# Attention scores from 64-row matmuls on undoubled operands, in a two-layer decoder kernel

## The chip, the cores and the metric

The kernel runs on one core of a Trainium2 chip. The metric is the device time of one execution in microseconds (us), the lower the better. One launch computes everything below.

## What is computed

Two decoder layers, for a prompt of 1024 tokens and for 8 sampled tokens with a paged cache. Each layer projects the normalized input and splits it over two groups of heads: four heads of differential attention and four heads of gated linear attention. Both groups feed one output projection, which a SwiGLU block follows. The change lies in the attention of the prompt. Each of its heads has two maps of queries and keys, 64 wide, and values 128 wide:

```python
def diff_attn_prompt(q, k, v, lam):
    ...
    scale = DIFF_DK ** -0.5
    ...
    def one_block(args):
        qi, i = args
        s = jnp.einsum('bqhmd,bkhmd->bhmqk', qi, k).astype(jnp.float32) * scale
        ...
        p = jax.nn.softmax(jnp.where(mask, s, -jnp.inf), axis=-1)
        w = p[:, :, 0] - lam * p[:, :, 1]
        return jnp.einsum('bhqk,bkhv->bqhv', w.astype(v.dtype), v)
```

Here `m` runs over the two maps, `q` over the queries of a block of 128, `k` over the keys, and the mask lets a query see the keys up to its own position.

## The kernel before

Each layer goes through three stages. `phase_d` does the differential attention of the prompt, `phase_g` the gated linear attention, and the last and longest stage the output projection and the feed-forward block in two halves, with the decoding of the samples mixed into the first. `phase_d` takes roughly the first 300 us of each layer.

To keep accuracy, matrices are split into a high part, rounded to the fast matmul format (F32R), and a low part, the rest. A product is then the sum of high times high, low times high and high times low. A projection (`gemm_tok`) does this with three matmuls for each of eight slices of the input.

In `phase_d`, each of the four heads prepares its weights (`prep_cols`: a copy on ScalarE, ACT, and a subtraction on VectorE, DVE) and then walks over eight tiles of 128 tokens and one of the samples. `proj(i)` projects tile i into the PSUM tile `psq`, normalizes and rotates queries and keys on ACT and DVE, transposes them on TensorE (PE) into the PSUM tile `tpqk`, and lays them out as operands: rows 0 to 63 come from map 0, rows 64 to 127 from map 1. `attend(i)` follows two tiles behind (`LAG`). It multiplies the queries of tile i with all keys up to tile i, in pieces of up to 512 keys, so tiles 0 to 3 have one piece and tiles 4 to 7 two. Each piece of a map goes into a PSUM tile `psS` of a pool of three (tag `S`), from which one DVE operation (line 504) adds the mask, scales, and keeps a running extreme in `mx`. ACT then takes the exponential of the row, the maps are combined, PE transposes the result (`tpw`, into `wT`) and multiplies it with the values (`po`, in full precision, two matmul instructions for each call).

The layout of the operands is where the change lies. A score of one map needs a contraction over 64 rows only. The kernel before fills all 128 rows of the array instead: `qhh` holds the high part of a map's queries twice, once in each half of the rows, and `kt` holds the high part of that map's keys in one half and the low part in the other. One matmul (line 500) then gives high times high plus high times low. A second one (line 501) takes the low part of the queries, `ql`, against the same keys. It is zero in the other half; for that, four tiles `qlz` are zeroed by GpSimd (POOL) at the start of the stage (lines 579 to 582) and only their live halves are written. So a piece of a map takes two matmuls of 128 rows, and a tile's operands take four ACT copies (lines 471, 475, 476, 481) and four DVE subtractions of 64 rows (lines 474, 482, 483).

The order on each engine isn't written out by hand in this stage. Instructions carry a priority in program order, and a planner places each engine's instructions before the launch by priority and readiness under its own estimate of durations. An instruction that isn't ready lets others pass it in the plan, and on the chip each engine then keeps to the plan. So matmuls of later projections stand between those of scores, transposes and `po`.

Two other matmuls of the kernel use less than the whole array and are spoken of below. `puG` in `phase_g` (line 794) writes 64 columns at a time, the lower and the upper half in turn, in full precision. `psw` in the decoding (line 1182) contracts over 64 rows and gives 32 columns of result.

Of the kernel before, what the change touches and what calls it, by code (L numbers as in the profile page):

```python
# [10 lines left out]
F32 = mybir.dt.float32  # L11
F32R = mybir.dt.float32r
# [3 lines left out]
AF = mybir.ActivationFunctionType  # L16
ALU = mybir.AluOpType
# [4 lines left out]
P = 128  # L22
DM = 1024
KD = DM // P
SEQ = 1024
# [15 lines left out]
DK = 64  # L41
# [3 lines left out]
LAG = 2  # L45
# [9 lines left out]
BIG = 3.0e38  # L55


def f(ap):
    return ap.bitcast(F32)
# [3 lines left out]
def hybrid_kernel(  # L63
# [8 lines left out]
    PE, ACT, DVE, POOL, SP = nc.tensor, nc.scalar, nc.vector, nc.gpsimd, nc.sync  # L72
# [8 lines left out]
    def mm(out, lhsT, rhs, start, stop):  # L81
        PE.matmul(out, lhsT=lhsT, rhs=rhs, start=start, stop=stop, skip_group_check=True)  # L82
# [4 lines left out]
    def act(out, in_, func, **kw):  # L87
        return ACT.activation(out, in_, func, **kw)  # L88
# [45 lines left out]
    def tt(out, a, b, op, eng=None):  # L134
        return (eng or DVE).tensor_tensor(out, a, b, op=op)  # L135
# [4 lines left out]
    def bc(ap, shape):  # L140
        return ap.to_broadcast(shape)
# [242 lines left out]
    def phase_d(l, dctx, sn, pgp):  # L384
# [8 lines left out]
        dp = Two()  # L393
# [9 lines left out]
        def head(h):  # L403
# [3 lines left out]
            kt = [None, None]  # L407
# [4 lines left out]
            def proj(i):  # L412
                n = P if i < NT else NB
                ps = psg.tile([P, 512], F32, name="psq", tag="g")
                gemm_tok(ps, nc_, Hs, Ls, i)
                if i == NT:
                    z = dp.tile([NB, 384 + RANK], F32, name="zs", tag="zs", bufs=1)
                    z2 = dp.tile([P, 512], F32, name="zs2", tag="sqo", bufs=1)[0:NB, :nc_]
                    DVE.tensor_copy(z2, ps[32:32 + NB, :nc_])
                    tt(z[:, :nc_], ps[0:NB, :nc_], z2, ALU.add)  # L420
                    src = z
                else:
                    src = ps
                qn = pp.tile([P, 256], F32, name="qn", tag="qn", bufs=2)
                ms = pp.tile([P, 4], F32, name="ms", tag="ms", bufs=2)
                for a in range(4):
                    act(qn[:n, a * DK:(a + 1) * DK], src[:n, a * DK:(a + 1) * DK], AF.Square, accum_out=ms[:n, a:a + 1])
                act(ms[:n], ms[:n], AF.Ln, scale=r2[:n, i:i + 1], bias=eps_t[:n])
                rs = pp.tile([P, 4], F32, name="rs", tag="rs", bufs=2)
                act(rs[:n], ms[:n], AF.Exp, scale=-0.5, bias=lnr[:n, i:i + 1])  # L430
                t2 = pp.tile([P, 256], F32, name="t2", tag="t2", bufs=1)
                qk = pp.tile([P, 256], F32, name="qk", tag="t1", bufs=2)
                v4 = "p (a d) -> p a d"
                v22 = "p (a m d) -> p a m d"
                vr = "p (a s d) -> p a s d"
                qs = src[:n, 0:256].rearrange(v22, a=2, m=2)
                tt(qk[:n].rearrange(v22, a=2, m=2), qs, bc(cg[:n, i, :, :].unsqueeze(2), [n, 2, 2, DK]), ALU.mult)
                tt(t2[:n].rearrange(v22, a=2, m=2), qs, bc(sg[:n, i, :, :].unsqueeze(2), [n, 2, 2, DK]), ALU.mult)
                tt(qk[:n].rearrange(vr, a=4, s=2), qk[:n].rearrange(vr, a=4, s=2),
                   t2[:n].rearrange(vr, a=4, s=2)[:, :, ::-1, :], ALU.add)  # L440
                tt(qk[:n].rearrange(v4, a=4), qk[:n].rearrange(v4, a=4), bc(rs[:n].unsqueeze(2), [n, 4, DK]), ALU.mult)
                v = dp.tile([P, DV], F32, name="v", tag="v", bufs=10)
                act(v[:n], src[:n, 256:384], AF.Copy, scale=rcol[:n, i:i + 1])
                if has_gr:
                    grt = pp.tile([P, RANK], F32, name="grt", tag="grt", bufs=2)
                    act(grt[:n], src[:n, 384:nc_], AF.Copy, scale=rcol[:n, i:i + 1])
                if i == NT:
                    if has_gr:
                        tp = psT.tile([P, 512], F32, name="tpgr", tag="T")
                        pe_t(tp[0:RANK, 0:NB], grt[0:NB], NB)  # L450
                        act(ssq[0:RANK, SEQ:TOK], tp[0:RANK, 0:NB], AF.Copy)
                    SP.dma_start(scr_q[l][:, h * P:(h + 1) * P], qk[:n, 0:128])
                    SP.dma_start(k_sample[l, :, h * P:(h + 1) * P], qk[:n, 128:256])
                    SP.dma_start(v_sample[l, :, h * P:(h + 1) * P], v[:n])
                    tt(z[:, 0:128], qk[:n, 0:128], qk[:n, 128:256], ALU.mult)
                    DVE.tensor_reduce(out=sn[:, 2 * h:2 * h + 2], in_=z[:, 0:128].rearrange("p (m d) -> p m d", m=2), axis=AX.X, op=ALU.add)
                    SP.dma_start(scr_v[l][:, h * P:(h + 1) * P], v[:n])
                    return None
                SP.dma_start(k_prompt[l, i * P:(i + 1) * P, h, :], qk[:, 128:256])
                SP.dma_start(v_prompt[l, i * P:(i + 1) * P, h, :], v)  # L460
                vts.append(v)
                tp = psT.tile([P, 512], F32, name="tpqk", tag="T")
                pe_t(tp[:, 0:128], qk[:, 0:128], P)
                pe_t(tp[:, 128:256], qk[:, 128:256], P)
                if has_gr:
                    pe_t(tp[0:RANK, 256:384], grt, P)
                    act(ssq[0:RANK, i * P:(i + 1) * P], tp[0:RANK, 256:384], AF.Copy)
                qhh = dp.tile([P, 2, P], F32R, name="qhh", tag="qhh", bufs=LAG + 2)
                ql = qlz[nql[0] % len(qlz)]
                nql[0] += 1  # L470
                act(qhh, bc(tp[:, 0:128].unsqueeze(1), [P, 2, P]), AF.Copy)
                for m in range(2):
                    r = slice(64 * m, 64 * m + 64)
                    tt(ql[r, m, :], tp[r, 0:128], f(qhh[r, m, :]), ALU.subtract)
                act(qhh[64:128, 0, :], tp[0:64, 0:128], AF.Copy)
                act(qhh[0:64, 1, :], tp[64:128, 0:128], AF.Copy)
                if i % 4 == 0:
                    kt[i // 4] = dp.tile([P, 2, 512], F32R, name="kt", tag="kt", bufs=3)
                kk = kt[i // 4]
                c = slice((i % 4) * P, (i % 4 + 1) * P)  # L480
                act(kk[:, :, c], bc(tp[:, 128:256].unsqueeze(1), [P, 2, P]), AF.Copy)
                tt(kk[64:128, 0, c], tp[0:64, 128:256], f(kk[0:64, 0, c]), ALU.subtract)
                tt(kk[0:64, 1, c], tp[64:128, 128:256], f(kk[64:128, 1, c]), ALU.subtract)
                qts[i] = (qhh, ql)

            wTs = []

            def attend(i):
                qhh, ql = qts.pop(i)
                n = (i + 1) * P  # L490
                sms = dp.tile([P, 2], F32, name="sms", tag="sms")
                scs = []
                for m in range(2):
                    sc = dp.tile([P, SEQ], F32, name="sc", tag="sc", bufs=4)
                    mx = dp.tile([P, 2], F32, name="mx", tag="mx", bufs=3)
                    for pi in range(0, n, 512):
                        w = min(512, n - pi)
                        ps = psS.tile([P, 512], F32, name="psS", tag="S")
                        kk = kt[pi // 512]
                        mm(ps[:, :w], qhh[:, m, :], kk[:, m, :w], True, False)  # L500
                        mm(ps[:, :w], ql[:, m, :], kk[:, m, :w], False, True)
                        o = SEQ - n + pi
                        q = pi // 512
                        DVE.tensor_tensor_reduce(
                            out=sc[:, pi:pi + w], in0=ps[:, :w], in1=mb[:, o:o + w], scale=-(DK ** -0.5),
                            scalar=BIG if q == 0 else mx[:, 0:1], op0=ALU.add, op1=ALU.min, accum_out=mx[:, q:q + 1])
                    q = (n - 1) // 512
                    act(sc[:, :n], sc[:, :n], AF.Exp, scale=-1.0, bias=mx[:, q:q + 1], accum_out=sms[:, m:m + 1])
                    scs.append(sc)
                rr = dp.tile([P, 2], F32, name="rr", tag="rr")  # L510
                DVE.reciprocal(rr, sms)
                tt(rr, rr, coef[:, l, :], ALU.mult)
# [63 lines left out]
        POOL.affine_select(out=mb[:, SEQ - P:], in_=mb[:, SEQ - P:], pattern=[[-1, P]], base=0,  # L576
                           channel_multiplier=1, compare_op=ALU.is_ge, fill=-1.0e30)

        nql = [0]
        qlz = [dp.tile([P, 2, P], F32R, name=f"qlz{z}", tag=f"qlz{z}", bufs=1) for z in range(LAG + 2)]  # L580
        for z in qlz:
            POOL.memset(f(z), 0.0)
        wa2 = pgp.tile([RANK, 256], F32, name="wa2", tag="wa2")
        POOL.dma_start(wa2, w_a2[l])
        pending = []
# [747 lines left out]
```

## Time and profile before

| | |
|---|---|
| median of three runs | 2788.39 us (2784.14 to 2790.25) |
| the profiled execution | 2795.14 us |
| its span, first to last instruction | 2793.3 us |
| mean granted clock of TensorE | 0.989 of full speed |
| PE busy | 2709.5 us, 97% of the span |
| ACT busy | 1358.8 us, 49% |
| DVE busy | 1824.9 us, 65% |
| POOL busy | 403.0 us, 14% |

A row of the profile names the line of the kernel (that of a helper, where one records the operation: L82 is every matmul, L85 every transpose, L88 every ACT operation, L135 a DVE operation on two tensors), the engine, the operation, and what is written and read by the program's names. PE is the matmul, PEld the load of its weights, which may run ahead of it. A matmul's shape is written as rows by columns of the array, then the size of what streams through it. The ends of matmuls are modelled: each lasts longer than the slot it takes in the stream, so successive ones overlap, and the distance between two starts is the better measure of what one costs. A row with a count in the timeline merges successive instructions of one kind, from the first start to the last end.

### The profile page before, as it was taken

What the parts mean: (1) busy time and instruction counts of PE and PEld (TensorE: products, weight loads), DVE (VectorE), ACT (ScalarE), POOL (GpSimd) and SP (SyncE); (2) the same over time, 40 slices, a digit from 0 to 9 for tenths busy, and PEclk for the clock granted to TensorE, in tenths of its full rate; (3) what the DMA queues carried; (4) which work ended last, traced back from release to release, by engine and by line L of the source; (5) the groups of instructions that cost most, each with busy time, mean ns of one, the idle gap of its engine ahead of it and who ended that gap; (6) DMA issues with size and microseconds to landing.
All of it is one profiled execution on the core that took longest, in us unless ns stands there. A gap on an engine that the chain in (4) does not pass through costs nothing.

```text
span 2793.3 us, 46822 instructions
## 1 busy us (share of the span) xinstructions
PE 2709.5 (97%) x16906; PEld 2403.9 (86%) x16906; DVE 1824.9 (65%) x3549; ACT 1358.8 (49%) x3343; POOL 403.0 (14%) x333
## 2 busy tenths in 40 slices
PE   8999999999999999999999999999999999999999
PEld 6888788777888799999988878877788888999999
DVE  6777676788777664444477775777777775544444
ACT  7888545533454442222278884455324454322222
POOL 1000100145343100000020001002453430000000
PEclk9999999999999999999999999999999999999999
DMA  5111111356666342333212111124566665333332
GB/s 133 56 56 41 57 32 54 109 176 201 185 200 195 104 128 84 93 94 94 75 42 70 47 38 49 32 59 137 174 202 177 191 192 151 91 92 91 91 91 84
DMA packets 461322, 298.13 MB, mean 107 GB/s; under 512 B 34698, under 2 KB 416906, under 8 KB 461090
## 3 DMA queue, kind: packets, MB, share of 16 engines
q1 hardware_dynamic: 452322, 290.90, 35.4%
q10 hardware_dynamic: 8704, 4.20, 0.6%
q8 instruction: 134, 2.20, 0.3%
q14 instruction: 98, 0.80, 0.1%
q0 software_dynamic: 64, 0.03, 0.0%
HBM read 271.53 MB, written 23.53 MB: 106 GB/s over the span
## 4 chain that ended last, share of the span: by engine, by line
PE 78%; DVE 10%; ACT 8%; issue 2%; DMA 2%; SPq 0%; POOL 0%; ACTq 0%; DVEq 0%; POOLq 0%
PE psd L82 56%; PE psq L82 4%; PE psqk L82 3%; PE psv L82 3%; PE psgg L82 2%; PE po L82 2%; ACT sc L88 2%; PE psA L82 1%; DVE wl L135 1%; PE psS L82 1%; ACT qn L88 1%; PE poG L82 1%; ACT qhh L88 1%; PE tpw L85 1%; DVE acc L135 1%
## 5 line engine op out<-in xcount | busy, mean ns | idle before, releaser
L88 ACT ACTIVATE wh<-raw 128x512 fp32r<-128x512 f32 (+1 forms) x608 | 353.6, 615 | 909.3 <-PE psd L82 737.3
L82 PE MATMUL psd<-xH,wh 128*128 128x260 f32 (+1 forms) x2112 | 681.9, 323 | 3.6 <-ACT xH L88 3.5
L82 PE MATMUL psd<-xL,wh 128*128 128x260 f32 (+1 forms) x2112 | 679.9, 322 | 4.2 <-DVE xL L138 4.2
L82 PE MATMUL psd<-xH,wl 128*128 128x260 f32 (+1 forms) x2112 | 682.2, 323 | 0.9 <-DVE wl L135 0.9
L135 DVE TENSOR_TENSOR wl<-raw,wh 128x512 fp32r<-128x512 f32 (+1 forms) x608 | 443.9, 746 | 72.8 <-issue 41.3
L82 PEld LDWEIGHTS psd<-xL,wh 128*128 128x128 f32 x2112 | 400.2, 189 | 38.4 <-DVE xL L138 6.5
L82 PEld LDWEIGHTS psd<-xH,wh 128*128 128x128 f32 x2112 | 399.8, 189 | 36.3 <-ACT xH L88 4.4
L82 PEld LDWEIGHTS psd<-xH,wl 128*128 128x128 f32 x2112 | 400.3, 190 | 34.2 <-DVE wl L135 1.8
L82 PE MATMUL psd<-hh,wl 128*128 128x260 f32 (+1 forms) x1056 | 340.6, 323 | 6.1 <-DVE wl L135 6.0
L82 PE MATMUL psd<-hh,wh 128*128 128x260 f32 (+1 forms) x1056 | 338.8, 321 | 0.9 <-DVE acc L135 0.9
L82 PE MATMUL psd<-hl,wh 128*128 128x260 f32 (+1 forms) x1056 | 338.3, 320 | 0.0
L135 POOL TENSOR_TENSOR page<-page,qbd 128x512 f32<-128x512 f32 x128 | 190.5, 1504 | 307.9 <-DMA page<-in_cache_k 162.7
L135 DVE TENSOR_TENSOR acc<-psd,acc 128x520 f32<-128x520 f32 (+1 forms) x144 | 125.6, 872 | 150.7 <-PE psd L82 150.7
L82 PEld LDWEIGHTS psd<-hh,wl 128*128 128x128 f32 x1056 | 199.1, 189 | 25.8 <-DVE wl L135 12.0
L82 PEld LDWEIGHTS psd<-hh,wh 128*128 128x128 f32 x1056 | 199.2, 189 | 14.6 <-issue 1.3
L82 PEld LDWEIGHTS psd<-hl,wh 128*128 128x128 f32 x1056 | 198.8, 188 | 13.6
L82 PE MATMUL psq<-wh,xH 128*128 128x384 f32 (+1 forms) x512 | 180.0, 352 | 7.3 <-DVE zs L135 4.3
L135 DVE TENSOR_TENSOR sa<-psd,rstd 128x520 f32<-128x520 f32 (+1 forms) x66 | 57.7, 874 | 197.0 <-PE psd L82 194.7
L82 PE MATMUL psq<-wh,xL 128*128 128x384 f32 (+1 forms) x512 | 179.4, 351 | 0.0
L82 PE MATMUL psq<-wl,xH 128*128 128x384 f32 (+1 forms) x512 | 178.6, 349 | 0.0
L135 DVE TENSOR_TENSOR tb<-psd,rstd 128x520 f32<-128x520 f32 (+1 forms) x66 | 57.7, 874 | 165.9 <-PE psd L82 165.9
L138 DVE SCALAR_TENSOR_TENSOR wl<-raw,g1c,wh 128x256 fp32r<-128x256 f32 (+2 forms) x160 | 80.9, 536 | 73.5 <-ACT wh L88 72.8
(330 smaller groups left out, 5421.2 us busy)
## 6 DMA issues: line engine op xcount, KB each, us to landing
raw<-in_w_gu SPq DMA_DIRECT2D x176, 512.0 KB
raw<-in_w_down SPq DMA_DIRECT2D x160, 256.0 KB
page<-in_cache_k SPq DMA_DIRECT2D x128, 256.0 KB
page<-in_cache_v SPq DMA_DIRECT2D x128, 256.0 KB
raw<-in_w_out SPq DMA_DIRECT2D x32, 512.0 KB
raw<-in_w_in SPq DMA_DIRECT2D x64, 192.0 KB
raw<-in_w_in SPq DMA_DIRECT2D x64, 128.0 KB
xt<-in_x_prompt SPq DMA_DIRECT2D x8, 512.0 KB
```

Source lines behind the costliest of these rows:

```text
L82: PE.matmul(out, lhsT=lhsT, rhs=rhs, start=start, stop=stop, skip_group_check=True)
L85: PE.matmul(out, lhsT=in_, rhs=ident[:n, :n], is_transpose=True)
L88: return ACT.activation(out, in_, func, **kw)
L135: return (eng or DVE).tensor_tensor(out, a, b, op=op)
L138: (eng or DVE).scalar_tensor_tensor(out=out, in0=in0, scalar=scalar, in1=in1, op0=op0, op1=op1)
```

## The change

Queries and keys are kept as they leave the transpose, once. `qk_t` holds the high part of both maps' queries in its first half and the low part in its second, `kt` the same for the keys. One ACT copy and one DVE subtraction over all 128 rows make each. A score piece of one map is now three matmuls over the 64 rows of that map: high times high, high times low, low times high. Both maps of a piece are done together, each with a `psS` tile of its own, their matmuls alternating between the lower and the upper half of the rows. The reductions, the exponentials and everything behind them stay, though the exponentials of both maps now come after all pieces. The zeroed tiles go.

```diff
--- before.py
+++ after.py
@@ -465,48 +465,43 @@
                 if has_gr:
                     pe_t(tp[0:RANK, 256:384], grt, P)
                     act(ssq[0:RANK, i * P:(i + 1) * P], tp[0:RANK, 256:384], AF.Copy)
-                qhh = dp.tile([P, 2, P], F32R, name="qhh", tag="qhh", bufs=LAG + 2)
-                ql = qlz[nql[0] % len(qlz)]
-                nql[0] += 1
-                act(qhh, bc(tp[:, 0:128].unsqueeze(1), [P, 2, P]), AF.Copy)
-                for m in range(2):
-                    r = slice(64 * m, 64 * m + 64)
-                    tt(ql[r, m, :], tp[r, 0:128], f(qhh[r, m, :]), ALU.subtract)
-                act(qhh[64:128, 0, :], tp[0:64, 0:128], AF.Copy)
-                act(qhh[0:64, 1, :], tp[64:128, 0:128], AF.Copy)
+                qk_t = dp.tile([P, 2, P], F32R, name="qhl", tag="qhh", bufs=LAG + 2)
+                act(qk_t[:, 0, :], tp[:, 0:128], AF.Copy)
+                tt(qk_t[:, 1, :], tp[:, 0:128], f(qk_t[:, 0, :]), ALU.subtract)
                 if i % 4 == 0:
                     kt[i // 4] = dp.tile([P, 2, 512], F32R, name="kt", tag="kt", bufs=3)
                 kk = kt[i // 4]
                 c = slice((i % 4) * P, (i % 4 + 1) * P)
-                act(kk[:, :, c], bc(tp[:, 128:256].unsqueeze(1), [P, 2, P]), AF.Copy)
-                tt(kk[64:128, 0, c], tp[0:64, 128:256], f(kk[0:64, 0, c]), ALU.subtract)
-                tt(kk[0:64, 1, c], tp[64:128, 128:256], f(kk[64:128, 1, c]), ALU.subtract)
-                qts[i] = (qhh, ql)
+                act(kk[:, 0, c], tp[:, 128:256], AF.Copy)
+                tt(kk[:, 1, c], tp[:, 128:256], f(kk[:, 0, c]), ALU.subtract)
+                qts[i] = qk_t
 
             wTs = []
 
             def attend(i):
-                qhh, ql = qts.pop(i)
+                qk_t = qts.pop(i)
                 n = (i + 1) * P
                 sms = dp.tile([P, 2], F32, name="sms", tag="sms")
-                scs = []
+                scs = [dp.tile([P, SEQ], F32, name="sc", tag="sc", bufs=4) for _ in range(2)]
+                mxs = [dp.tile([P, 2], F32, name="mx", tag="mx", bufs=4) for _ in range(2)]
+                for pi in range(0, n, 512):
+                    w = min(512, n - pi)
+                    pss = [psS.tile([P, 512], F32, name="psS", tag="S") for _ in range(2)]
+                    kk = kt[pi // 512]
+                    for a, b in ((0, 0), (0, 1), (1, 0)):
+                        for m in range(2):
+                            r = slice(64 * m, 64 * m + 64)
+                            mm(pss[m][:, :w], qk_t[r, a, :], kk[r, b, :w], a + b == 0, a == 1)
+                    o = SEQ - n + pi
+                    q = pi // 512
+                    for m in range(2):
+                        mx = mxs[m]
+                        DVE.tensor_tensor_reduce(
+                            out=scs[m][:, pi:pi + w], in0=pss[m][:, :w], in1=mb[:, o:o + w], scale=-(DK ** -0.5),
+                            scalar=BIG if q == 0 else mx[:, 0:1], op0=ALU.add, op1=ALU.min, accum_out=mx[:, q:q + 1])
+                q = (n - 1) // 512
                 for m in range(2):
-                    sc = dp.tile([P, SEQ], F32, name="sc", tag="sc", bufs=4)
-                    mx = dp.tile([P, 2], F32, name="mx", tag="mx", bufs=3)
-                    for pi in range(0, n, 512):
-                        w = min(512, n - pi)
-                        ps = psS.tile([P, 512], F32, name="psS", tag="S")
-                        kk = kt[pi // 512]
-                        mm(ps[:, :w], qhh[:, m, :], kk[:, m, :w], True, False)
-                        mm(ps[:, :w], ql[:, m, :], kk[:, m, :w], False, True)
-                        o = SEQ - n + pi
-                        q = pi // 512
-                        DVE.tensor_tensor_reduce(
-                            out=sc[:, pi:pi + w], in0=ps[:, :w], in1=mb[:, o:o + w], scale=-(DK ** -0.5),
-                            scalar=BIG if q == 0 else mx[:, 0:1], op0=ALU.add, op1=ALU.min, accum_out=mx[:, q:q + 1])
-                    q = (n - 1) // 512
-                    act(sc[:, :n], sc[:, :n], AF.Exp, scale=-1.0, bias=mx[:, q:q + 1], accum_out=sms[:, m:m + 1])
-                    scs.append(sc)
+                    act(scs[m][:, :n], scs[m][:, :n], AF.Exp, scale=-1.0, bias=mxs[m][:, q:q + 1], accum_out=sms[:, m:m + 1])
                 rr = dp.tile([P, 2], F32, name="rr", tag="rr")
                 DVE.reciprocal(rr, sms)
                 tt(rr, rr, coef[:, l, :], ALU.mult)
@@ -576,10 +571,6 @@
         POOL.affine_select(out=mb[:, SEQ - P:], in_=mb[:, SEQ - P:], pattern=[[-1, P]], base=0,
                            channel_multiplier=1, compare_op=ALU.is_ge, fill=-1.0e30)
 
-        nql = [0]
-        qlz = [dp.tile([P, 2, P], F32R, name=f"qlz{z}", tag=f"qlz{z}", bufs=1) for z in range(LAG + 2)]
-        for z in qlz:
-            POOL.memset(f(z), 0.0)
         wa2 = pgp.tile([RANK, 256], F32, name="wa2", tag="wa2")
         POOL.dma_start(wa2, w_a2[l])
         pending = []
```

## Rows read from the trace of the kernel before

**Rows 1.** Busy us by stage: a steady head, a layer's last head

```profile
core 0: us, PE busy (x) PEld busy (x) DVE busy (x) ACT busy (x) POOL busy (x), PEclk, DMA share, GB/s
1499.36:1563.76 64.40, 62.85 (x347) 53.95 (x347) 51.63 (x156) 56.85 (x202) 0.00 (x0) 1.00 0.20 59
1631.37:1693.23 61.86, 55.89 (x292) 47.36 (x293) 46.39 (x142) 53.21 (x188) 2.03 (x5) 0.97 0.19 54
```

**Rows 2.** Matmul groups of the steady head (busy us, mean ns | idle before)

```profile
L82 PE MATMUL psq<-wh,xL 128*128 128x384 f32 x62 | 21.6, 348 | 0.0
L82 PE MATMUL po<-wT,v 128*128 128x256 f32 x32 | 7.9, 390 | 0.5 <-ACT wT L88 0.4
L85 PE MATMUL tpw<-ident,sc 128*128 128x128 f32 x36 | 5.7, 281 | 0.6 <-ACT wT L88 0.4
```

**Rows 3.** PE's timeline in the steady head (start us, us)

```profile
1533.19 0.39 PE L82 MATMUL psS<-kt,qlz 128*128 128x512 f32 x1
1533.42 0.28 PE L82 MATMUL psS<-kt,qhh 128*128 128x256 f32 x1
1533.54 0.28 PE L82 MATMUL psS<-kt,qlz 128*128 128x256 f32 x1
...
1534.13 0.34 PE L82 MATMUL psq<-wh,xH 128*128 128x384 f32 x1
1534.30 0.34 PE L82 MATMUL psq<-wh,xL 128*128 128x384 f32 x1
...
1557.69 1.03 PE L85 MATMUL tpw<-ident,sc 128*128 128x128 f32 x8
1558.98 3.51 PE L82 MATMUL po<-wT,v 128*128 128x256 f32 x16
```

**Rows 4.** Copies on ACT and DVE in the steady head, by shape

```profile
L88 ACT ACTIVATE qhh<-tpqk 64x128 fp32r<-64x128 f32 x16 | 4.3, 271 | 0.4 <-DVE qlz L135 0.2
L88 ACT ACTIVATE kt<-tpqk 128x256 fp32r<-128x256 f32 x8 | 3.1, 384 | 0.1
L88 ACT ACTIVATE qhh<-tpqk 128x256 fp32r<-128x256 f32 x8 | 3.0, 380 | 0.0
L88 ACT ACTIVATE wT<-tpw 128x128 f32<-128x128 f32 x2 | 0.5, 272 | 0.0
L135 DVE TENSOR_TENSOR qlz<-tpqk,qhh 64x128 fp32r<-64x128 f32 x17 | 4.9, 287 | 4.6 <-ACT qhh L88 4.2
L135 DVE TENSOR_TENSOR kt<-tpqk,kt 64x128 fp32r<-64x128 f32 x16 | 4.6, 288 | 2.1 <-ACT kt L88 1.7
```

**Rows 5.** PE's timeline around layer 0's first puG, first two alone

```profile
365.23 0.40 PE L82 MATMUL psqk<-xL,wh 128*128 128x512 f32 x1
365.46 0.40 PE L82 MATMUL psqk<-xH,wl 128*128 128x512 f32 x1
365.79 0.44 PE L82 MATMUL puG<-gv,gkT 128*64 128x128 f32 x4
366.16 0.50 PE L82 MATMUL psqk<-xH,wh 128*128 128x512 f32 x1
366.50 0.40 PE L82 MATMUL psqk<-xL,wh 128*128 128x512 f32 x1
...
365.79 0.33 PE L82 MATMUL puG<-gv,gkT 128*64 128x128 f32 x2
```

**Rows 6.** PE's timeline around layer 0's psw

```profile
735.36 0.39 PE L82 MATMUL psd<-hh,wh 128*128 128x512 f32 x1
735.68 1.08 PE L82 MATMUL psw<-sel,dpe 64*128 64x32 f32 x8
736.69 0.51 PE L82 MATMUL psd<-hl,wh 128*128 128x512 f32 x1
737.12 0.74 PE L82 MATMUL psw<-sel,dpe 64*128 64x32 f32 x5
```

**Rows 7.** Waits of the steady head (us, times, longest)

```profile
PEld psS L82 <- DVE mx L504: 1.3, 4, 0.5
```

## The prediction

> **What bounds the kernel now.** The change lies in phase_d alone, which runs twice for some 300 us, four heads each. I read the busy times by stage first, for one head in steady state and for the last head of a layer. In a steady head of 64.40 us PE is busy 62.85 us, ACT 56.85 and DVE 51.63, at full granted clock [rows 1]. So PE leads, with ACT close behind, and neither DMA nor POOL matters here.
>
> PE's busy time overstates the work, since the ends of matmuls overlap. So I read the spacing of starts next: a 512-wide matmul takes 0.23 us of the queue, a 256-wide one 0.12, a 384-wide projection 0.17 to 0.175, a 128-wide transpose 0.107 ((1.03 - 0.28) / 7), one of the 256-wide po matmuls 0.208 ((3.51 - 0.39) / 15) [rows 2, 3]. What one head needs of PE: 192 projections, 33.0 us, and 16 for the samples, 2.7; 32 po at 0.208 and 8 half as wide, 7.5; 36 tpw and 16 tpqk transposes at 0.107, 5.6; the four norm matmuls about 1.7 (an estimate, twice a po each). The scores: six pieces of 512 columns and two each of 384, 256 and 128, for two maps, two matmuls each, so 24 x 0.23 + 8 x (0.175 + 0.12 + 0.11) = 8.8. Together 59.3 us, so about 5 us of 64.40 are true stalls. In the last head PE is idle 5.97 us by the busy times against 1.55, so some 9.5 us are stalls there [rows 1]. For both layers: 6 x 5 + 2 x 9.5 = 49 us of stall. That is all that relief elsewhere can ever give back.
>
> **Part 1, the copies.** Per token tile ACT loses one 128x256 copy into qhh (0.380 us), two half copies (0.271 each) and the 128x256 copy into kt (0.384), and gets two 128x128 copies, which the 128x128 copy out of PSUM prices at 0.272 [rows 4]. That is 1.31 us out, 0.54 in: 0.76 less per tile, 6.1 per head, 11% of ACT's 56.85. DVE loses four 64-row subtractions of 0.287 and gets two of 128 rows over the same 128 columns. No such row stands in the trace; the 64-row one bounds it below at 0.287, and two of them above at 0.574, where nothing is gained. I take 0.29, since the ACT rows show the 128-row copy at the price of the 64-row one: 4.6 us per head less. None of this is PE work. It helps only where PE waits for these engines, and it shortens the way from transpose to operands by about 0.9 us. The zeroed ql tiles and their POOL fills cost nothing either way.
>
> **Part 2, the matmuls.** Each piece of scores goes from four 128-row matmuls to six 64-row ones, alternating upper and lower half. No row of before shows two row halves side by side. The nearest is puG, whose matmuls use 64 columns of the array, alternating halves: two of the four, started with it, last 0.33 us together, and all four 0.44 [rows 5]. One after the other, at 0.107 each, four would last about 0.6. So halves do run side by side, at least by columns. I take that for rows too: a piece then streams three times its width instead of four. Fully unpaired it would be six times.
>
> The Trainium skill, TensorE: Matmul & The Clock Gate, Part 3, says the same of row groups and gives 3.07x for four tiles. By that alone the sum would be 2.2 us less per head.
>
> **Part 3, the switch.** Against it stands what happens around every run of half-array matmuls. The 512-wide psqk before puG gives way after 0.33 us (365.46 to 365.79) instead of 0.23, and the one behind it takes 0.34 (366.16 to 366.50) [rows 5]. It is the same around psw, which uses 64 rows: psd gives way after 0.32 us (735.36 to 735.68). The last psw starts at about 736.49 (735.68 + 1.08 - 0.27), and psd only 0.20 later, where the psw follow each other at 0.11. That psd then takes 0.43, up to the next psw [rows 6], which is its 0.23, the 0.09 of the next change, and 0.11 for weights that weren't loaded ahead. So a change of array shape costs 0.09 us of draining and about 0.11 of exposed weight load, twice per run: 0.40 us for each unbroken run of half-array matmuls. Where PE would have stalled anyway, it costs nothing: the bounds of one run are 0 and 0.40.
>
> The Trainium skill has this rule in TensorEngine Tiling (Array Packing), Key Properties: changing the tiling mode drains the engine. The rows agree and give its price.
>
> So even a perfectly paired piece loses as a run by itself. With 512 columns it takes 0.40 + 3 x 0.23 = 1.09 us where it took 0.92; with 256 it takes 0.76 for 0.48, with 128 0.73 for 0.44. Only two pieces in one run break even.
>
> How many runs? Tiles 0 to 3 have one piece, tiles 4 to 7 two. psS has three buffers, and today PE already waits for the DVE reductions that free them, 1.3 us in this head [rows 7]. A pair takes two buffers, so the second piece gets one at once and the other only after a reduction. I expect its two maps to fall apart: three matmuls of map 0 behind the first piece, three of map 1 later, with other 128-row work between them. That makes 8 + 4 = 12 runs per head, 4.8 us. Streaming: the eight first pieces paired save 5 x 0.23 + 0.175 + 0.12 + 0.11 = 1.56 us; the four second pieces unpaired cost 2 x (0.23 + 0.175 + 0.12 + 0.11) = 1.27 more. The sum on PE is +4.5 us per head. The bounds: all paired and merged into 8 runs, -2.2 + 3.2 = +1.0; nothing paired in 12 runs, 3.1 + 1.3 + 4.8 = +9.2. In every case PE needs more than before.
>
> **The sum.** Eight heads x 4.5 = +36 us. I let one switch in five fall into a stall, 8 x 1.0 = -8. The relief of ACT and DVE I put at 2 us per head, -16, a third of the 49 us of stalls. Its ends are 0, if the stalls are mere latency, and some two thirds, 32 us. Net +12. The profiled run took 2795.1 us around a span of 2793.3, 0.24% above the median of 2788.4; phase_d is the same work in each, so I add to the median: about 2801. The case's own range is 2785 to 2820.
>
> **Rivals.**
> (1) The relief wins; this is the mechanism that ends faster. In phase_d ACT is 88% busy and works in order, so each late copy delays the transposes and po behind it. If two thirds of the stalls go (-32) and all pieces pair in 12 runs (8 x 2.6 = +21), the net is -11, 2777; merged into 8 runs (+8) it is -24, 2764. For it: PE's waits name ACT and DVE. Against it: only 5 us per steady head are there to be won. It decides from the point where the relief exceeds 4 us per head.
> (2) Pairing doesn't happen, because row halves serialize or because the order on PE tears the maps apart. Then 9.2 x 8 = 74, less 8 and 16: +50, 2838. For it: no row shows row halves together, and the order of PE's queue mixes other matmuls in. Against it: puG.
> (3) The edit does on PE nothing that matters: switches hidden in waits, relief off the path; 2784 to 2794. For it: 1.3 us of the waits in a head stand right before score matmuls.
>
> **How the numbers follow.** Forecast 0.50 (0.40 of it slower by over 0.2%, 0.10 within), rival 1 0.25, rival 2 0.17, rival 3 0.08 (0.01 of it faster). 0.2%, some 5.6 us, is about what a measurement of this kernel can tell from no change. Faster 0.26, same 0.17, slower 0.57. The range reaches into rivals 1 and 2: 2770 to 2838, and takes in the bounds of a run and of the relief.
>
> **What would show it.** In the profile after: psS as 576 matmuls of 64 rows, starting two by two within some 0.01 us if paired; about 96 unbroken runs of them or somewhat more; 0.3 us or more between a 512-wide matmul and a score run behind it; the copies at 0.27 and 0.29 us; ACT's busy time 49 us less and DVE's 37 less over the span; nothing changed outside phase_d. A steady head is about 66 us long if I am right, under 63 if the relief wins, over 70 if nothing pairs. I would be wrong above all if the switches cost less for row halves than for psw, or if runs of a whole tile stay unbroken.

## The result

The changed kernel takes 2825.5 us, the kernel before 2787.6 in the same rounds: a ratio of 1.0127, 95% interval 1.0113 to 1.0142, some 35 us slower (the medians differ by 38; all differences below are taken from ratios). The forecast was slower, with 2801 us, 12 us more than before; the measured loss is almost three times that.

The loss lies in `phase_d`. The timeline of PE, cut to the last three `po` of each layer, first two of the kernel before, then two of the changed one (start us, us):

```profile
306.26 0.60 PE L82 MATMUL po<-wT,v 128*128 128x256 f32 x3
1692.63 0.60 PE L82 MATMUL po<-wT,v 128*128 128x256 f32 x3
```

```profile
321.81 0.60 PE L82 MATMUL po<-wT,v 128*128 128x256 f32 x3
1721.34 0.60 PE L82 MATMUL po<-wT,v 128*128 128x256 f32 x3
```

They come 15.5 us later in layer 0 and another 13 us later in layer 1. The stages behind keep their lengths to within a few us. The head of the page after the change (busy us, share, count of instructions):

```profile
span 2824.2 us, 46886 instructions
...
PE 2748.8 (97%) x17098; PEld 2404.8 (85%) x17098; DVE 1772.0 (63%) x3421; ACT 1323.7 (47%) x3215; POOL 401.3 (14%) x325
```

ACT is busy 35 us less and DVE 53 us less than before, although the program takes longer. PE is busy 39 us more, with 192 matmuls more. The busy times by stage of a steady head, against [rows 1]:

```profile
core 0: us, PE busy (x) PEld busy (x) DVE busy (x) ACT busy (x) POOL busy (x), PEclk, DMA share, GB/s
1574.70:1644.80 70.10, 69.18 (x380) 55.81 (x379) 45.71 (x138) 54.04 (x189) 0.00 (x0) 1.00 0.13 40
```

This head takes 70.1 us, and PE's busy time fills 69.2 of it. It is cut at another point of the head than the 64.4 us of [rows 1]; from last `po` to last `po`, the head of [rows 1] goes from 64.4 to 69.6 us. ACT has 2.8 us less to do than in the head of before, DVE 5.9 less. (Heads differ in how much of the next head's weights they prepare, so these aren't the copies alone.) The copies, against [rows 4]:

```profile
L88 ACT ACTIVATE qhl<-tpqk 128x128 fp32r<-128x128 f32 x8 | 2.2, 270 | 0.8 <-PE tpqk L85 0.6
L88 ACT ACTIVATE kt<-tpqk 128x128 fp32r<-128x128 f32 x8 | 2.2, 269 | 1.0 <-DVE qhl L135 1.0
...
L135 DVE TENSOR_TENSOR qhl<-tpqk,qhl 128x128 fp32r<-128x128 f32 x8 | 2.3, 289 | 4.5 <-ACT qhl L88 4.5
L135 DVE TENSOR_TENSOR kt<-tpqk,kt 128x128 fp32r<-128x128 f32 x8 | 2.3, 286 | 0.8 <-ACT kt L88 0.7
```

They came out as priced: 0.27 us each on ACT, 0.29 on DVE. Over the whole trace the copies take 49 us less of ACT (83.2 to 34.3) and 37 less of DVE (73.6 to 36.8), as predicted; the page's busy times differ from that because they count the time in which instructions overlap once. Next the timeline of PE around the scores of a tile with one piece of 512 keys (start us, us):

```profile
203.06 0.34 PE L82 MATMUL psq<-wh,xL 128*128 128x384 f32 x1
203.24 0.34 PE L82 MATMUL psq<-wl,xH 128*128 128x384 f32 x1
203.50 0.96 PE L82 MATMUL psS<-kt,qhl 64*128 64x512 f32 x6
204.40 0.44 PE L82 MATMUL psq<-wh,xH 128*128 128x384 f32 x1
204.68 0.34 PE L82 MATMUL psq<-wh,xL 128*128 128x384 f32 x1
204.85 0.34 PE L82 MATMUL psq<-wl,xH 128*128 128x384 f32 x1
```

The six matmuls take 0.96 us from the first start to the last end. One after the other, the five slots of 0.23 before the last one's start would alone be 1.15. They run in pairs. But psq gives way after 0.26 us before the run (203.24 to 203.50) where its slot is 0.17, and the one behind the run takes 0.28 (204.40 to 204.68). From 203.42, when the next matmul was due, to 204.51, where the stream is back in step, are 1.09 us: the prediction's 0.40 + 3 x 0.23. One price, as in [rows 5, 6], and it was right. The weight loads of the same stretch show where part of it goes:

```profile
203.07 0.19 PEld L82 LDWEIGHTS psq<-wl,xH 128*128 128x128 f32 x1
203.50 0.53 PEld L82 LDWEIGHTS psS<-kt,qhl 64*128 64x128 f32 x6 [0.25 <-issue]
204.40 0.19 PEld L82 LDWEIGHTS psq<-wh,xH 128*128 128x128 f32 x1 [0.37 <-issue]
```

A psq load starts 0.17 us ahead of its matmul (203.07 and 203.24). The first load of the run and the first behind it start with theirs (203.50, 204.40).

What was not expected to this extent is how the work is cut up. The same view some microseconds later:

```profile
208.94 0.34 PE L82 MATMUL psq<-wl,xH 128*128 128x384 f32 x1
209.22 0.49 PE L82 MATMUL psS<-kt,qhl 64*128 64x512 f32 x2
209.78 0.66 PE L85 MATMUL tpw<-ident,sc 128*128 128x128 f32 x4
210.37 0.79 PE L82 MATMUL psS<-kt,qhl 64*128 64x512 f32 x5
211.21 1.78 PE L82 MATMUL po<-wT,v 128*128 128x256 f32 x8
212.92 0.33 PE L82 MATMUL psS<-kt,qhl 64*128 64x128 f32 x2
213.27 0.41 PE L85 MATMUL tpqk<-ident,qk 128*128 128x128 f32 x2
213.61 0.43 PE L82 MATMUL psS<-kt,qhl 64*128 64x128 f32 x3
```

Two score matmuls, four transposes, five score matmuls, eight `po`, two scores, two transposes, three scores: four runs where the prediction had two. Counted over PE's whole timeline there are 144 unbroken runs of score matmuls, 18 per head, 22 of them of a single matmul. The price shows as well in the idle time of the weight loads, from 60 to 280 us in layer 0 (busy us, mean ns | idle before, what ended it):

```profile
L82 PEld LDWEIGHTS psq<-wh,xH 128*128 128x128 f32 x203 | 38.2, 188 | 4.5 <-issue 3.1
L82 PEld LDWEIGHTS psS<-kt,qhl 64*128 64x128 f32 x222 | 23.4, 184 | 13.6 <-issue 7.2 <-DVE mx L499 1.3 <-ACT kt L88 1.0
```

7.2 us of idle time before the score loads and 3.1 before those of a third of the projections are put down to "issue": the engine waited for nothing that the profile shows.

### The profile page after: what moved, and what is told of

Read it like the earlier page. It is cut to its first block, busy times and chain, and to the rows that moved or that the text cites. A ratio compares the mean times of both kernels' runs of the same rounds, so it can differ in the third digit from the quotient of the medians.

```text
span 2824.2 us, 46886 instructions
## 1 busy us (share of the span) xinstructions
PE 2748.8 (97%) x17098; PEld 2404.8 (85%) x17098; DVE 1772.0 (63%) x3421; ACT 1323.7 (47%) x3215; POOL 401.3 (14%) x325
## 4 chain that ended last, share of the span: by engine, by line
PE 84%; DVE 9%; ACT 3%; issue 2%; DMA 2%; POOL 0%; SPq 0%; ACTq 0%; DVEq 0%; POOLq 0%
PE psd L82 56%; PE psq L82 8%; PE psqk L82 3%; PE psS L82 3%; PE psv L82 3%; PE psgg L82 2%; PE po L82 2%; DVE wl L135 1%; PE tpw L85 1%; PE psA L82 1%; PE poG L82 1%; DVE acc L135 1%; DVE gD L135 1%; DMA raw<-in_w_in 1%; PE tpqk L85 1%
```

## The experiments

The theory: a change of the array's shape costs about 0.40 us of PE's stream per unbroken run of half-array matmuls; the row halves do pair; the cheap copies give something back. Rival A: the loss comes from the order and the buffers (both maps at once, two psS tiles out of three). Rival B: the relief of ACT and DVE is worth nothing, or pairs gain nothing.

**Relief alone.** The operands of the changed kernel, in place of four ACT copies and four DVE subtractions of 64 rows, under the matmuls of before:

```diff
...
+  act(qhh[:, 0, :], tp[:, 0:128], AF.Copy)
+  tt(qhh[:, 1, :], tp[:, 0:128], f(qhh[:, 0, :]), ALU.subtract)
+  act(kk[:, 0, c], tp[:, 128:256], AF.Copy)
+  tt(kk[:, 1, c], tp[:, 128:256], f(kk[:, 0, c]), ALU.subtract)
-  mm(ps[:, :w], qhh[:, m, :], kk[:, m, :w], True, False)
-  mm(ps[:, :w], ql[:, m, :], kk[:, m, :w], False, True)
+  mm(ps[:, :w], qhh[:, 0, :], kk[:, m, :w], True, False)
+  mm(ps[:, :w], qhh[:, 1, :], kk[:, m, :w], False, True)
```

> The kernel before with the cheap copies of the changed one: two ACT copies and two DVE subtractions of 128 rows per tile, and its own two 128-row matmuls per piece and map, in its own order (125 unbroken runs of score matmuls on PE, 123 before). The matmuls take natural operands, so the scores are sums over both maps: that part of the computation is changed. Theory (a change of array shape costs about 0.4 us per run, the copies give a little back): faster than before by 8 to 16 us, about 2776. Rival A (the loss comes from the order with both maps at once): the same here. Rival B (the copies' relief is worth nothing, or puts the planner's order wrong): within 5 us of before.

Measured: 0.9931 (0.9918 to 0.9944), 19 us faster. The relief is real, and a little larger than the 16 us that the prediction took and the 8 to 16 expected here.

**Matmuls alone.** The changed kernel with copies as many and as wide as before, for the queries as shown and for the keys likewise:

```diff
-  act(qk_t[:, 0, :], tp[:, 0:128], AF.Copy)
-  tt(qk_t[:, 1, :], tp[:, 0:128], f(qk_t[:, 0, :]), ALU.subtract)
+  act(qk_t, bc(tp[:, 0:128].unsqueeze(1), [P, 2, P]), AF.Copy)
+  for m in range(2):
+      r = slice(64 * m, 64 * m + 64)
+      tt(qk_t[r, 1, :], tp[r, 0:128], f(qk_t[r, 0, :]), ALU.subtract)
+  act(qk_t[0:64, 0, :], tp[0:64, 0:128], AF.Copy)
+  act(qk_t[64:128, 0, :], tp[64:128, 0:128], AF.Copy)
...
```

> The changed kernel, but with as many and as wide copies and subtractions as before (two ACT copies of 128x256, two of 64 rows, four DVE subtractions of 64 rows per tile, some writing the same values again). PE's order has 137 runs of score matmuls, the changed kernel's 144. Theory: the switches alone, so slower than before by 38 to 50 us, about 2832, and slower than the changed kernel by 3 to 12. Rival B (relief worth nothing): equal to the changed kernel within 4 us.

Measured: 1.0158 (1.0143 to 1.0173), 44 us slower than before, 9 us slower than the changed kernel. So the cheap copies are worth 19 us under the old matmuls and only 9 under the new ones.

**Order and buffers.** The changed kernel, its loops and copies, but over all 128 rows:

```diff
-  for a, b in ((0, 0), (0, 1), (1, 0)):
+  for a in range(2):
       for m in range(2):
-          r = slice(64 * m, 64 * m + 64)
-          mm(pss[m][:, :w], qk_t[r, a, :], kk[r, b, :w], a + b == 0, a == 1)
+          mm(pss[m][:, :w], qk_t[:, a, :], kk[:, m, :w], a == 0, a == 1)
```

> The changed kernel with its cheap copies, its order of loops and its two psS tiles at once, but each map's three 64-row matmuls replaced by two over all 128 rows (the scores are then sums over both maps: that part is changed). Theory (array shape): no switches, so faster than before by 5 to 16 us, about 2778, 45 us below the changed kernel. Rival A (order and buffers: two psS tiles at once out of three, exponentials after all pieces): still slower than before by 15 to 30 us.

Measured: 0.9938 (0.9923 to 0.9952), 17 us faster than before. Rival A falls: both maps at once cost nothing. Between this kernel and the changed one lie 0.0189, or 53 us, and the difference is in the score matmuls. The weight loads of the same stretch as above, in this kernel:

```profile
L82 PEld LDWEIGHTS psq<-wh,xH 128*128 128x128 f32 x211 | 39.7, 188 | 1.4 <-issue 0.7
L82 PEld LDWEIGHTS psS<-kt,qhl 128*128 128x128 f32 x178 | 30.0, 189 | 6.2 <-DVE mx L498 3.4 <-ACT rs L88 0.4 <-ACT qhl L88 0.2
```

The idle time put down to "issue" has gone: none is among the three largest before the scores, 0.7 us stands before the projections.

**One lone run per projection.** In the kernel before, one of the 24 matmuls of a projection over half its rows:

```diff
-  mm(ps[:, :n], xH[:, k, ts], Ls[k][:, :n], False, k == KD - 1)
+  r = slice(0, 64) if k == 3 else slice(0, P)
+  mm(ps[:, :n], xH[r, k, ts], Ls[k][r, :n], False, k == KD - 1)
```

> The kernel before; in each projection of a token tile with 24 matmuls, one (the last of slice 3) contracts over rows 0 to 63 alone, so half of one term is left out. 64 of these in phase_d and 32 in phase_g, the streaming unchanged. Theory: 96 lone runs at 0.40 us, 38 us, or 30 if one in five falls into a stall: about 2818 to 2826. Rivals A and B: no difference to before.

Measured: 1.0063 (1.0048 to 1.0078), 18 us. The timeline of PE around one of them, in `phase_g`:

```profile
333.07 0.28 PE L82 MATMUL psv<-wh,xH 128*128 128x256 f32 x1
333.19 0.29 PE L82 MATMUL psv<-wh,xL 128*128 128x256 f32 x1
333.41 0.38 PE L82 MATMUL psv<-wl,xH 64*128 64x256 f32 x1
333.72 0.39 PE L82 MATMUL psv<-wh,xH 128*128 128x256 f32 x1
333.94 0.28 PE L82 MATMUL psv<-wh,xL 128*128 128x256 f32 x1
```

Where 256-wide matmuls follow each other at 0.12 us, the steps here are 0.22, 0.31 and 0.22: 0.39 us more than three of 0.12. In the stream the price is as forecast, in the time only half of it arrives, 0.19 us per run. The same in the kernel with cheap copies:

> The run lone_half again (96 lone 64-row matmuls in the projections), now in the kernel of the run relief_only, with its cheap copies and changed scores. The 96 cost 19 us there, half of the 0.40 that each takes of the stream. If the other half was hidden by stalls of PE which the cheap copies take away: 64 in phase_d at 0.30 to 0.37 and 32 in phase_g at 0.2, 26 to 30 us above relief_only, ratio to before 1.003 to 1.004. If it was hidden otherwise: 19 us again, ratio 1.000.

Measured: 1.0022 (1.0010 to 1.0033), 0.0091 or 25 us above `relief_only` (expected 26 to 30). The 96 runs cost more where the stalls have gone. That fits the reading that stalls of PE had hidden them, and that relief and switches don't add because each takes the same stalls. The sums of PE's steps below bear it out.

**Pairs.** The three matmuls of one map ahead of those of the other:

```diff
-  for a, b in ((0, 0), (0, 1), (1, 0)):
-      for m in range(2):
+  for m in range(2):
+      for a, b in ((0, 0), (0, 1), (1, 0)):
```

> The changed kernel with the three matmuls of map 0 ahead of the three of map 1, so that neighbours stand in the same half of the rows. PE's order has 122 runs of score matmuls instead of 144. Theory: the same work streams six widths a piece where pairs streamed three; from all paired to none would be 35 + 17 = 52 us, and 179 of 288 possible pairs were real, so about 33 us more, less 22 runs at 0.37, 8 us: slower than the changed kernel by about 25 us, ratio to before 1.022. Rival B (pairs gain nothing): 8 us faster than the changed kernel, ratio about 1.010.

Measured: 1.0161 (1.0143 to 1.0180), about 10 us above the changed kernel, between the two expectations, and for a reason that neither had: the edit didn't undo the pairs. The timeline of PE, cut just behind the start of one run's second matmul:

```profile
230.99 0.50 PE L82 MATMUL psS<-kt,qhl 64*128 64x512 f32 x2
```

Two matmuls of 512 columns together last 0.50 us, a lone first one 0.49: the second started 0.01 us after the first. In PE's order, as in the program's, the first three of this run belong to map 0, so what started beside the first is the first of map 1, the fourth in that order. PE lets each half of the rows go on by itself. Counted by starts, 168 pairs are left of 179, so this run says little on the value of pairs. It is 10 us slower than the changed kernel, with 22 runs fewer, because PE waits more. Here is what the weight loads of the scores wait for in layer 0 (us, times, longest), first in this kernel, then in the changed one; in layer 1 it is the same:

```profile
PEld psS L82 <- DVE mx L499: 4.8, 8, 0.6
```

```profile
PEld psS L82 <- DVE mx L499: 2.0, 7, 0.6
```

This is one of several waits that grew; the sums of PE's steps below give the whole.

Putting both maps on one half does undo the pairs, in the same PE order:

```diff
-  r = slice(64 * m, 64 * m + 64)
+  r = slice(0, 64)
```

> The changed kernel with the matmuls of both maps over rows 0 to 63 (map 1 repeats map 0's scores: that part is changed), so no two can stand side by side. PE's order is that of the changed kernel, 144 runs. Theory (pairs are real and worth their streaming time): 179 pairs of some 0.18 us are undone, 32 us if nothing hides them, 22 to 32 us above the changed kernel, ratio to before 1.020 to 1.024. Rival B (pairs gain nothing): equal to the changed kernel, 1.013.

Measured: 1.0233 (1.0217 to 1.0249), 0.0106 or 30 us above the changed kernel, as expected if pairs are real. The 512-wide score matmuls over the whole trace, first this kernel's, then the changed one's:

```profile
L82 PE MATMUL psS<-kt,qhl 64*128 64x512 f32 x288 | 95.8, 448 | 1.5 <-DVE mx L499 1.5
```

```profile
L82 PE MATMUL psS<-kt,qhl 64*128 64x512 f32 x288 | 71.3, 451 | 1.8 <-DVE mx L499 1.8
```

PE is busy 24.5 us longer with the same 288 matmuls.

**The number of runs.** First by holding runs together. Both maps of a piece share a two-bank tile; of these there are two; for that `psg`, the pool of the projections' `psq` tiles, gives up one of its three banks, and the kernel before gets the same shares as a control (`before_banks`, with four psS tiles of one bank):

```diff
-  psS = ...(tc.tile_pool(name="psS", bufs=3, ...))
+  psS = ...(tc.tile_pool(name="psS", bufs=2, ...))
-  psg = ...(tc.tile_pool(name="psg", bufs=3, ...))
+  psg = ...(tc.tile_pool(name="psg", bufs=2, ...))
-  pss = [psS.tile([P, 512], F32, name="psS", tag="S") for _ in range(2)]
+  pss2 = psS.tile([P, 2, 512], F32, name="psS", tag="S")
+  pss = [pss2[:, m, :] for m in range(2)]
```

`two_bank` is that and no more. `few_runs` and `one_run` also issue all matmuls of a piece, or of a tile, behind its first, at a priority ahead of everything else.

> The kernel before with four psS tiles instead of three and two psg instead of three, the bank shares of the run one_run. Every theory: a control; within 6 us of before either way. If it is faster or slower by more, that share is taken off one_run.

> The banks of before_banks and one_run (two psS tiles of two banks, two psg), both maps of a piece in one psS tile, but the matmuls not held together: 108 runs of score matmuls against 62 in one_run, nearly all paired. Theory: 46 runs more at 0.3 to 0.4 us, 14 to 18 us above one_run, ratio to before about 1.015 to 1.016. Rival (the number of runs doesn't matter): equal to one_run, 1.010.

> As two_bank, but the six matmuls of a piece are held together, 86 runs of 6 or 12, all paired. Theory: 24 runs above one_run, 7 to 10 us, ratio about 1.013. Rival (the number of runs doesn't matter): equal to one_run, 1.010.

> The changed kernel with its score matmuls held together: both maps of a piece share a two-bank psS tile (two of them, psg cut from three to two), a tile's matmuls, 6 or 12, are issued behind the first of them and ahead of everything else, and the first is the one whose operand is ready last. PE's order has 62 runs, all of 6 or 12. Theory: 17 us of relief and 17 us of streaming gained (three widths for four), 62 runs at 0.37, 23 us, lost: about 11 us faster than before, ratio 0.996, within 0.990 to 1.003. Rival A (order and buffers) or a rival in which each 64-row matmul costs more, however it is grouped: no better than the changed kernel, 1.010 to 1.015.

Measured: the control 1.0099 (1.0080 to 1.0118), against expectation 28 us slower by the banks alone; 108 runs 1.0098 (1.0083 to 1.0114); 86 runs 1.0088 (1.0072 to 1.0103); 62 runs 1.0097 (1.0076 to 1.0118). All four agree. Here the number of runs decides nothing, and `one_run`, all paired and with cheap copies, only equals its control where it should have been 11 us faster. PE's waits in layer 0 (us, times, longest), first of the kernel before, then of the control, then of `one_run`:

```profile
PE tpw L85 <- DVE sc L138: 3.1, 7, 1.1
```

```profile
PE tpw L85 <- DVE sc L138: 7.1, 8, 2.4
```

```profile
PE tpw L85 <- DVE sc L138: 8.3, 12, 2.0
PE psq L82 <- DVE zs L135: 4.0, 2, 2.0
PE psq L82 <- ACT v L88: 3.4, 3, 2.8
```

With one psg tile less, PE runs out of projections to do while it waits for the DVE step ahead of the transposes: 3.1 us before, 7.1 in the control, 8.3 in `one_run`, and there 7.4 more on the copies that free psq tiles (1.7 before, none in the control). These rows name only part of the 28 us. Where PE waits like this, switches can fall into the waits. The steps of PE say that they do: in `phase_d` the steps around runs lose 54, 46 and 40 us with 108, 86 and 62 runs, and the other waits, with stretches of a lower clock, 66, 70 and 81, so the sum hardly moves (the reckoning is that of the table below). So this group doesn't measure the price of a run, and the question was put again without touching banks or order.

**Shape alone.** `full_rows` again, instruction for instruction in the same PE order, with fewer rows, first as in `half_rows` (the first added line), then as in `half_by_turns` (the two behind it):

```diff
-  mm(pss[m][:, :w], qk_t[:, a, :], kk[:, m, :w], a == 0, a == 1)
+  mm(pss[m][:, :w], qk_t[0:64, a, :], kk[0:64, m, :w], a == 0, a == 1)
+  r = slice(0, 64) if m == 0 else slice(0, P)
+  mm(pss[m][:, :w], qk_t[r, a, :], kk[r, m, :w], a == 0, a == 1)
```

> The run full_rows with all 384 score matmuls over rows 0 to 63 instead of all 128 (the scores are then those of map 0, without parts of the product: changed, as in full_rows). PE's order is instruction for instruction that of full_rows, nothing can pair, and the streaming is the same; only the array's shape changes, in 125 runs. A price per run of 0.30 to 0.40 us: 38 to 50 us above full_rows, ratio to before 1.007 to 1.012. The order as cause: equal to full_rows, 0.994.

> The run full_rows with the 192 score matmuls of map 0 over rows 0 to 63 and those of map 1 over all rows, in the same PE order: half as many 64-row matmuls as half_rows, but in 154 runs, since the maps take turns. A price per run: 46 to 62 us above full_rows, ratio 1.010 to 1.016, above half_rows by 9 to 12 us. A price per 64-row matmul: half of half_rows' surplus, ratio 1.001 to 1.003. The order as cause: equal to full_rows.

Measured: 1.0067 (1.0050 to 1.0084) and 1.0075 (1.0057 to 1.0093), 36 and 38 us above `full_rows`. Same order, same streaming, nothing paired: the shape alone costs 36 us in 125 runs, 0.29 each. Half as many 64-row matmuls in 154 runs cost no less, 0.25 per run. A price per matmul would have halved it. But 29 runs more should have cost 9 to 12 us more, and they cost 2 (with an interval of some 7 us either way), so in the time no fixed price per run comes out. The weight loads of `half_rows`, in the stretch used above:

```profile
L82 PEld LDWEIGHTS psS<-kt,qhl 64*128 64x128 f32 x156 | 24.1, 185 | 13.9 <-issue 8.8 <-DVE mx L498 1.6 <-ACT ms L88 0.3
```

The idle time put down to "issue" is back, 8.8 us, with the order of `full_rows`. So the switches are shown as the main cause, at 0.25 to 0.29 us of the time per run where PE is nearly full.

**Where PE's steps go.** The traces tell what became of the rest. A step of PE lasts from one start to the next. The table adds up its steps in both layers, from the first projection of `phase_d` to the last `po`. The usual slot of each matmul is taken off by its width (0.23 us for 512 columns, 0.175 for 384, 0.12 for 256, 0.11 for 128, 0.216 for a 256-wide `po`; a pair counts once). What is left is parted into the steps around runs of 64-row matmuls (into the run, its first, out of it, and the one behind), those in stretches with a granted clock of 0.50, and all others, for the most part waits (all in us and rounded, one profiled execution each):

| kernel | steps in all | slots | around runs | other waits | at 0.50 |
|---|---|---|---|---|---|
| before | 587 | 509 | 0 | 74 | 4 |
| `lone_half` | 597 | 509 | 26 | 56 | 6 |
| `full_rows` | 562 | 508 | 0 | 51 | 3 |
| `half_rows` | 603 | 507 | 46 | 35 | 15 |
| `half_by_turns` | 609 | 508 | 58 | 32 | 11 |
| changed | 616 | 512 | 57 | 38 | 9 |
| `no_pairing` | 622 | 514 | 49 | 58 | 2 |

The steps around runs come to 0.39 to 0.41 us per run in each of them, once the runs at 0.50 are left out. So the price in the stream is that of the prediction; waits that shrink beside it hide part of it, 18 us in `lone_half` and 13 to 19 where the copies are cheap. `half_by_turns` loses 12 us more around its runs than `half_rows`, and 6 less in the two columns behind. `no_pairing` loses 8 less around its runs than the changed kernel, and 20 more in other waits.

The last column is the clock, which no experiment held fixed. Here is PE before and in the last such stretch of layer 0, in the changed kernel, and below the same time in the kernel before (busy us, granted clock behind them):

```profile
284.80:294.80 10.00, 8.56 (x52) 7.17 (x52) 5.56 (x19) 7.22 (x25) 0.00 (x0) 1.00 0.19 47
294.80:308.50 13.70, 13.70 (x33) 7.84 (x32) 7.38 (x26) 6.32 (x14) 0.00 (x0) 0.50 0.11 29
```

```profile
284.80:294.80 10.00, 8.57 (x43) 6.48 (x43) 9.16 (x32) 8.93 (x21) 0.00 (x0) 1.00 0.16 42
294.80:306.60 11.80, 10.15 (x58) 8.50 (x57) 6.59 (x15) 9.20 (x18) 0.00 (x0) 1.00 0.27 72
```

In the changed kernel PE goes on at 0.50 of its clock (1.2 GHz) for 13.7 us; in the kernel before, as busy in the ten us ahead, it stays at 1.00. Why it fell is not shown. It weighs most in `half_rows`: of the 41 us by which its steps exceed those of `full_rows`, 12 are at 0.50.

**A version that beats both.** The relief can be had without a change of shape. The kernel before, with the two half copies of the queries on POOL, which has little to do in this stage:

```diff
-  act(qhh[64:128, 0, :], tp[0:64, 0:128], AF.Copy)
-  act(qhh[0:64, 1, :], tp[64:128, 0:128], AF.Copy)
+  POOL.tensor_copy(qhh[64:128, 0, :], f(qhh[0:64, 0, :]))
+  POOL.tensor_copy(qhh[0:64, 1, :], f(qhh[64:128, 1, :]))
```

> The kernel before, its matmuls and operands unchanged, with the two half copies of queries made by POOL out of the high operand in SBUF instead of by ACT out of PSUM: 0.54 us less of ACT per tile, 35 us in all, where relief_only took 49 us from ACT and 37 from DVE and gained 17. Theory (relief without a change of array shape is pure gain): 4 to 10 us faster than before, ratio 0.9965 to 0.9985. Rival (POOL is slow on it, or stands in DVE's way): same as before or slower.

Measured: 0.9973 (0.9963 to 0.9984), 7.5 us faster than the kernel before and about 43 us than the changed one. It computes the whole product, as `relief_only` and `full_rows` do not.

## Why the prediction was right in kind and short in size

- **What bounds `phase_d`.** Right: the stage followed PE's stream. Relief alone won 19 us of the 49 that the prediction had as stalls. One of its readings was a little low: the 16 `po` in its row include two half as wide, so a full one takes 0.216 us and not 0.208, some 0.3 us per head, which the sum doesn't feel.
- **The copies.** Right in price. Relief was put at 16 us; it is 19 alone, and 9 beside the new matmuls. Here the sum failed to see that switches and relief feed on the same stalls, a matter of 7 us.
- **Pairs.** Right in number: 179 of the 288 possible pairs were real, against 192 forecast, and undoing them costs 30 us. Which ones was not as forecast: of 48 pairs of 384 columns only 20 were real, where the one-piece tiles alone would give 24. Its sign "over 70 us if nothing pairs" misled, since the steady head reached 70 with these pairs; the runs were too many, not the pairs too few.
- **The price of a run.** Right in the stream: 0.40 us in the prediction, 0.39 in `lone_half`, 1.09 us for a paired 512 piece as forecast, and 0.39 to 0.41 per run in the table. What reaches the time is half of it in the kernel before, and 0.25 to 0.29 us where the copies are cheap. "One in five falls into a stall" was too little cover for the lone runs, where 18 of 26 us were hidden.
- **The number of runs.** This is the term that was mis-sized. The prediction derived 12 runs per head from pieces and buffers, 96 in all, and took the planner's mixing for a remark. There are 144, and the steps around them come to 57 us, or 62 with those at 0.50, where 96 at 0.40 gave 38. The trace before could have told: its score matmuls, with no shape to keep together, already stood in 123 unbroken runs, 15 per head. With 144 runs at 0.40, one in five covered, 2 us saved in streaming and 16 us of relief, the same sum gives 144 x 0.40 x 0.8 - 2 - 16 = +28, near the measured 35; at 96 it gave +12. That it comes so near is partly luck: against the table, streaming cost 3 us instead of saving 2, the stretches at 0.50, which the prediction put at nothing, cost 5 more than before, and the waits shrank by 36 us, where this sum takes 28.
- **What stays open.** From `full_rows` to the changed kernel are 53 us in the time and 54 in the table: 57 around the runs, 6 at 0.50, 4 of slots, less 13 of waits that shrank. Why the clock fell where it did, and why the waits shrink by as much as they do, was not found. The table rests on one execution of each kernel.
- **The rivals.** The relief's win failed on the switches, though relief by itself was larger than the forecast took. That row halves serialize was excluded by `same_half`. The other half of that rival, an order on PE that tears the maps apart, came true in part: it left 109 of 288 pairs undone, where 96 were forecast, and made the runs 144.

## What to carry to other kernels

Matmuls over half the array paid here for each change of shape, 0.40 us of PE's stream per unbroken run, part of it in weight loads that weren't ahead of their matmul. Count the unbroken runs in the planned order of PE, not the pieces in the source, and multiply; then ask how much of it PE's waits will hide. Where the order couldn't be kept together without taking buffers from something else, full-array matmuls on doubled operands were cheaper here. The cost of making such operands could be moved to an engine that idles, which gave the only gain of a kernel that computes the whole product.

## What the runs showed of the hardware

- Matmuls on the two row halves run side by side even when they aren't neighbours in the program: in `no_pairing` the fourth of the order started 0.01 us after the first. In that kernel 108 pairs start 10 ns apart; with alternating loops, in the changed kernel, 157 start 3 or 4 ns apart. For pairing the loops needn't alternate.
- A copy by ACT of 128x128 out of PSUM takes as long as one of 64x128, 0.270 against 0.271 us, and a DVE subtraction 0.289 against 0.287. Two half copies cost two whole ones.
- Giving one of three projection tiles in PSUM to the scores cost 28 us, against 35 for the change itself, with the same instructions. Of that, 4 us lie in stretches at 0.50 of the clock, by the reckoning of the table.
